# A small extra store on every DMA engine at the start of a scaling kernel

## The chip, the cores and the metric

The kernel runs on one core of a Trainium2 chip. A core has several engines that run side by side, each with its own queue of instructions. Three of them matter here: DVE (VectorE) and ACT (ScalarE) compute, and SP (SyncE) only issues transfers. ACT issues transfers too, from the same queue as its arithmetic. The transfers themselves are carried out by 16 DMA engines, which move data between the chip's large memory (HBM) and the core's own memory (SBUF, 128 partitions).

The metric is the device time in microseconds of one execution. The time before is a median of 240.64 us over four runs, which lie between 239.93 and 241.71. A profile shows one further execution in detail.

## The reference

Each of 16 x 1024 tokens has a row of 512 numbers and two weights. The output holds the row twice, once multiplied by each weight. The expert indices are an input, but nothing is computed from them.

```python
batch, seq, hidden, n_experts = 16, 1024, 512, 8
k = 2
x_expanded = x[:, :, np.newaxis, :].repeat(k, axis=2)
weights = expert_weights[..., np.newaxis]
return (x_expanded * weights).astype(np.float32)
```

All numbers are float32. So 33.5 MB are read, 67.1 MB are written, and there are two multiplications for each number read.

## The kernel before

The tokens are seen as one list of 16384 rows. They are cut into eight tiles of 2048 tokens. In a tile, partition p holds 16 consecutive tokens, so that one partition's share of a load of x is one run of 32 KB in HBM. A load of x is therefore 128 pieces of 32 KB, eight for each DMA engine.

The weights of all tiles stand in one small tile of SBUF, `w_tile`. It is filled by eight loads of 16 KB, one for each tile of tokens (line 55). SP issues them. Each is 128 pieces of 128 bytes, again eight for each DMA engine.

The function `load` (line 69) issues the load of one tile of x from ACT's queue (line 76). Two buffers hold x, so the first two loads are issued before the main loop, and the load for tile i + 2 follows the work on tile i.

For each token position t of a tile, DVE multiplies by the first weight (line 97) and ACT by the second (line 91). Both write into `o_tile`, which holds 8 of the 16 positions. When it is full, SP issues a product store of 4 MB (line 105). That is again 128 pieces of 32 KB. There are 16 product stores, and four buffers for `o_tile`.

The source gives no explicit order between the engines. A planner lays out one instruction list for each engine. Among the instructions of an engine it takes the earliest one in the source that is ready; an instruction that still waits for another engine's result can so be passed by a later one. It also puts in the waits. Each transfer raises a completion counter when its last bytes have landed. There are eight such counters, and the transfers take them in turn, in the order in which the planner laid them out: first load of x, eight weights loads, second load of x, first product store, and so on. A transfer that takes a counter first waits until the transfer which had that counter before it has landed. Between the first few transfers, which are issued at once, these waits are the only ones.

The change is put between the definition of `rows` (line 46) and the list of weights loads (line 51).

Of the kernel before, what the change touches and what calls it, by code (L numbers as in the profile page):

```python
# [1 line left out]

# [4 lines left out]


@with_exitstack
def kernel(  # L10
    ctx: ExitStack,
    tc: tile.TileContext,
    x: bass.AP,
    expert_indices: bass.AP,
    expert_weights: bass.AP,
    out: bass.AP,
):
    nc = tc.nc

    batch, seq, hidden = x.shape  # L20
    k = expert_weights.shape[-1]
    P = nc.NUM_PARTITIONS
    ntok = batch * seq
    assert ntok % P == 0
    A_TOTAL = ntok // P

    f32 = mybir.dt.float32
    row = k * hidden
    TX = 16
    TO = 8  # L30


    groups = [[16], [16], [16], [16], [16], [16], [16], [16]]
    assert sum(sum(g) for g in groups) == A_TOTAL

    xf = x.rearrange("b s h -> (b s) h")
    of = out.rearrange("b s k h -> (b s) (k h)")
    wf = expert_weights.rearrange("b s k -> (b s) k")

    w_pool = ctx.enter_context(tc.tile_pool(name="w_pool", bufs=1))  # L40
    x_pool = ctx.enter_context(tc.tile_pool(name="x_pool", bufs=2))
    o_pool = ctx.enter_context(tc.tile_pool(name="o_pool", bufs=4))

    w_tile = w_pool.tile([P, A_TOTAL * k], f32)

    def rows(of_all, done, T):
        return of_all[done * P : (done + T) * P, :].rearrange(
            "(p a) n -> p (a n)", a=T
        )

    weights = []
    for group in groups:
        weights.append((sum(n for _, n in weights), sum(group)))
    for at, T in weights:
        nc.sync.dma_start(out=w_tile[:, at * k : (at + T) * k], in_=rows(wf, at, T))

    tiles = []
    done = 0
    for group in groups:
        T = sum(group)  # L60
        a0 = 0
        for n in group:
            tiles.append((done, T, a0, n))
            a0 += n
        done += T

    loaded = []

    def load(i):
        if i >= len(tiles):  # L70
            return
        done, T, a0, n = tiles[i]
        x_tile = x_pool.tile([P, TX * hidden], f32)
        cols = rows(xf, done, T)[:, a0 * hidden : (a0 + n) * hidden]
        for lo, hi in [(0, P)]:
            nc.scalar.dma_start(out=x_tile[lo:hi, : n * hidden], in_=cols[lo:hi, :])  # L76
        loaded.append(x_tile)

    for i in range(2):
        load(i)  # L80
    for i, (done, T, a0, n) in enumerate(tiles):
        x_tile = loaded[i]
        outr = rows(of, done, T)
        for t in range(n):
            if t % TO == 0:
                o_tile = o_pool.tile([P, TO * row], f32)
            for kk in range(k):
                c = (done + a0 + t) * k + kk
                o = t % TO * row + kk * hidden
                if kk == 1:  # L90
                    nc.scalar.mul(  # L91
                        out=o_tile[:, o : o + hidden],
                        in_=x_tile[:, t * hidden : (t + 1) * hidden],
                        mul=w_tile[:, c : c + 1],
                    )
                    continue
                nc.vector.tensor_scalar(  # L97
                    out=o_tile[:, o : o + hidden],
                    in0=x_tile[:, t * hidden : (t + 1) * hidden],
                    scalar1=w_tile[:, c : c + 1],  # L100
                    scalar2=None,
                    op0=mybir.AluOpType.mult,
                )
            if (t + 1) % TO == 0:
                nc.sync.dma_start(
                    out=outr[:, (a0 + t + 1 - TO) * row : (a0 + t + 1) * row],
                    in_=o_tile,
                )
        load(i + 2)

# [1 line left out]
_INS = ['x', 'expert_indices', 'expert_weights']  # L112
_OUTS = [((16, 1024, 2, 512), 'float32')]


# [23 lines left out]
```

## Time and profile before

| what | value |
|---|---|
| median of four runs | 240.64 us |
| the four runs | 239.93, 240.16, 241.13, 241.71 us |
| the profiled execution | 241.42 us |
| its span, first to last instruction | 239.6 us |
| DVE busy | 52.0 us in 128 multiplications, 482 ns each |
| ACT busy | 81.3 us, of it 128 multiplications of 708 ns and one table load of 1283 ns |
| read from HBM, written to HBM | 33.69 MB, 67.11 MB |
| a load of x, issue to landing | 23.4 us in the median |
| a weights load, issue to landing | 21.5 us in the median |
| a product store, issue to landing | 48.6 us in the median |

In the profile, q1 is SP's transfer queue and q10 is ACT's. Lines that start with DMA or GB/s cut the span into 40 equal slices, here of 6 us each. The digit is the busy share of the DMA engines in tenths, where 9 means 90% or more. "SPq" and "ACTq" are the issuing instructions of SP and ACT. The chain lists, in order of time, what the end of the program waited for: start, duration, what it was. The packet records of the trace hold start, duration, queue and size of every packet that a DMA engine moved. A transfer's piece is one packet, and each DMA engine adds a packet of 4 bytes at the end of its share, which raises the counter.

### The profile page before, as it was taken

To read this page: it belongs to the slowest core of one execution; us is meant where nothing else is said; L and a number is where in the kernel's file an instruction comes from. 1 tells how busy PE (TensorE), PEld (TensorE's weight loads), DVE (VectorE), ACT (ScalarE), POOL (GpSimd) and SP (SyncE) were. 2 spreads that over 40 slices of the span, in tenths; PEclk is the share of its full clock that TensorE was granted. 3 is DMA by queue.
4 is the path that set the end of the run, shared out by engine and by line. 5 is a ranking of instruction groups with operands and counts; after the bars stand their busy time and mean duration, and the time that the engine had idled before them with its cause. 6 is when DMAs were issued, how large, how long until landed. Compare 5 with 4: busy or idle time off the path is not lost.

```text
span 239.6 us, 384 instructions
## 1 busy us (share of the span) xinstructions
DVE 52.0 (22%) x128; ACT 81.3 (34%) x129; POOL 0.2 (0%) x4
## 2 busy tenths in 40 slices
DVE  0073910055005005050140502205041135000000
ACT  0279970085207108070170802507043165200000
POOL 0000000000000000000000000000000000000000
DMA  7999999999999999999999999999999999999994
GB/s 265 439 434 366 439 438 438 432 438 438 416 432 416 418 421 438 432 438 438 427 438 427 432 427 416 427 427 432 438 438 438 438 438 438 427 438 438 438 438 202
DMA packets 4610, 100.81 MB, mean 421 GB/s; under 512 B 1536, under 2 KB 1536, under 8 KB 1536
## 3 DMA queue, kind: packets, MB, share of 16 engines
q1 hardware_dynamic: 3456, 67.24, 65.3%
q10 hardware_dynamic: 1152, 33.55, 33.2%
q14 instruction: 2, 0.02, 0.0%
HBM read 33.69 MB, written 67.11 MB: 421 GB/s over the span
## 4 chain that ended last, share of the span: by engine, by line
DMA 48%; another core or an unknown queue 21%; ACT 16%; ACTq 1%; issue 1%
DMA out_dram<-o_tile 38%; ACT o_tile L91 16%; DMA x_tile<-in_x_dram 7%; DMA w_tile<-in_expert_weights_dram 3%; ACTq L76 1%; ACTq L134 0%; ACTq L91 0%
## 5 line engine op out<-in xcount | busy, mean ns | idle before, releaser
L91 ACT ACTIVATE o_tile<-x_tile,w_tile 128x512 f32<-128x512 f32 x128 | 80.0, 708 | 114.9 <-DMA out_dram<-o_tile 96.8
L97 DVE TENSOR_SCALAR o_tile<-x_tile,w_tile 128x512 f32<-128x512 f32 x128 | 52.0, 482 | 151.5 <-DMA out_dram<-o_tile 116.3
L91 ACT ACT_TABLE_LOAD x1 | 1.3, 1283 | 9.0 <-DMA w_tile<-in_expert_weights_dram 9.0
L123 POOL MEMSET const-uint8-127<- 128x1 uint8 x1 | 0.1, 102 | 0.0
L123 POOL MEMSET const-bfloat16-1.0<- 128x1 bf16 x1 | 0.1, 101 | 0.0
L123 POOL MEMSET const-float32-0.0<- 128x1 f32 x1 | 0.1, 98 | 0.2 <-issue 0.2
L123 POOL MEMSET const-float32-1.0<- 128x1 f32 x1 | 0.1, 98 | 0.0
## 6 DMA issues: line engine op xcount, KB each, us to landing
out_dram<-o_tile SPq DMA_DIRECT2D x16, 4096.0 KB, 48.6
x_tile<-in_x_dram ACTq DMA_DIRECT2D x8, 4096.0 KB, 23.4
w_tile<-in_expert_weights_dram SPq DMA_DIRECT2D x8, 16.0 KB, 21.5
```

What stands on the lines that cost most here:

```text
L76: nc.scalar.dma_start(out=x_tile[lo:hi, : n * hidden], in_=cols[lo:hi, :])
L91: nc.scalar.mul(out=o_tile[:, o : o + hidden], in_=x_tile[:, t * hidden : (t + 1) * hidden], mul=w_tile[:, c : c + 1],)
L97: nc.vector.tensor_scalar(out=o_tile[:, o : o + hidden], in0=x_tile[:, t * hidden : (t + 1) * hidden], scalar1=w_tile[:, c : c + 1], scala ...
L123: nc = _bacc.Bacc("TRN2", target_bir_lowering=False, num_devices=1)
```

## The change

A tile of 16 x 128 numbers is set to zero on DVE. SP stores it into the output before the weights loads in the source. The destination is the first 512 bytes of rows 0, 128, 256 and so on up to 1920. The 16 rows are shared out to the 16 DMA engines, so each engine gets one piece of 512 bytes. All these rows belong to the first tile of tokens, and the first product store writes them later with the products.

```diff
         return of_all[done * P : (done + T) * P, :].rearrange(
             "(p a) n -> p (a n)", a=T
         )
+
+
+
+    early = w_pool.tile([16, 128], f32)
+    nc.vector.memset(early, 0.0)
+    nc.sync.dma_start(
+        out=of[: P * TX, :128].rearrange("(e t) n -> e t n", e=16)[:, 0, :], in_=early
+    )
 
     weights = []
     for group in groups:
```

Nothing is removed. The eight weights loads, the loads of x, the arithmetic and the product stores stand in the source as before.

## The prediction

> **What bounds the kernel now.** I read the page's slices first, then its queues, then the chain that ended last, then the start alone.
>
> ```profile
> span 239.6 us, 384 instructions
> DVE 52.0 (22%) x128; ACT 81.3 (34%) x129; POOL 0.2 (0%) x4
> DMA  7999999999999999999999999999999999999994
> GB/s 265 439 434 366 439 438 438 432 438 438 416 432 416 418 421 438 432 438 438 427 438 427 432 427 416 427 427 432 438 438 438 438 438 438 427 438 438 438 438 202
> q1 hardware_dynamic: 3456, 67.24, 65.3%
> q10 hardware_dynamic: 1152, 33.55, 33.2%
> ```
>
> The DMA engines are busy in every slice but parts of the first and last. No compute engine passes 34%. The packet records say the same: 192 packets of 32 KB on each of the 16 engines, nearly all 1.213 us long, make 192 x 1.213 = 232.9 us. The first packet starts at 1.74 and the last ends at 238.49, so 236.8 us lie between them and only some 3.9 us are not plain copying. A change of 8 KB in 100 MB can only work on those 3.9 us, and the slices say where: the fourth, about 18 to 24 us, moves 366 GB/s where its neighbours move 439.
>
> The chain of waits in order of time shows what sets the start:
>
> ```profile
> 0.73 7.83 DMA w_tile<-in_expert_weights_dram
> 8.56 0.02 issue
> 8.59 15.90 DMA x_tile<-in_x_dram
> 24.49 0.02 issue
> 24.51 0.20 ACT o_tile L91
> 24.71 0.04 issue
> 24.75 0.33 ACTq L76
> ```
>
> The second load of x (ACT's queue, line 76) is not issued until the first weights load has landed at 8.56. It does not need the weights. It waits because transfers take eight completion counters in turn, and a counter's next transfer waits for its previous one: in the trace the first x load raises counter 99, the first seven weights loads 100 to 106, the eighth takes 99 again, and the second x load takes 100, the first weights load's. The sync queue's waits show the other case, the eighth weights load waiting for x:
>
> ```profile
> SPq L105 <- DMA w_tile<-in_expert_weights_dram: 10.5, 2, 6.0
> SPq L55 <- DMA x_tile<-in_x_dram: 8.9, 1, 8.9
> ```
>
> The stages of the start (time, then busy times, clock, DMA share, GB/s; a packet counts where it starts) show the loss:
>
> ```profile
> 13.50:20.80 7.30, 6.39 (x16) 7.30 (x12) 0.00 (x0) 1.00 1.01 432
> 20.80:22.40 1.60, 0.00 (x0) 1.60 (x4) 0.00 (x0) 1.00 1.26 329
> 22.40:23.20 0.80, 0.00 (x0) 0.80 (x2) 0.00 (x0) 1.00 0.34 49
> 23.20:24.80 1.60, 0.29 (x1) 0.46 (x2) 0.00 (x0) 1.00 1.66 648
> 24.80:60.00 35.20, 12.65 (x32) 18.24 (x30) 0.00 (x0) 1.00 1.00 432
> ```
>
> From 20.8 each engine's last x packet is stretched: 16 packets, mean 2.00 instead of 1.213 us, so **0.79 us** lost (2.49, so 1.28, on the engine that is furthest behind). Then come the weights packets that had piled up: on that engine 48 small ones from 24.13 to 24.60, **0.46 us** at some 9.5 ns each. Then stores begin.
>
> **Why they pile up.** Packet by packet, each engine takes one from SP's queue and one from ACT's. A small packet thus pays for a large one: after about five that pass before x flows, the first weights load (8 packets and one for its counter, per engine) needs four x packets, and its counter packets run from 7.40 to 8.22. The Trainium skill (DMA: Bandwidth & Descriptors, Queues, rings and completion order) also says round robin by packet, but with some 9 to 17 descriptors drained per packet. Then nine would pass in one turn; here they take one turn each, 1.22 us apart, and I use the row.
>
> **The change, part by part.**
>
> *The memset* on DVE: the nearest rows are the 0.10 us memsets on POOL and DVE's 0.48 us multiply of 128x512; I take 0.2. DVE is idle until 13.46, so nothing waits. Were that cover gone it would cost 0.2.
>
> *The store's place.* The planner takes per engine what is ready first: in the chain above, ACT's multiply at 24.51 stands ahead of the load at 24.75, which the source has earlier. At the start the first weights load is ready and the store is not (memset), so I expect the store second on SP, issued near 1.2 with the memset done. The other weights loads issue one issue time (0.33 to 0.74 us) later; they are far behind in their queue anyway, so 0.
>
> *Its own packets*: two per engine (512 bytes and a counter), 0.02 + 0.01 = **+0.03**.
>
> *The counters move by one.* First x load 99, first weights load 100, the store 101, and then the second x load, now the eleventh transfer, comes to 101: it waits for the store. The seventh weights load now waits for the first x load, as the eighth did; both then follow near 13.5 to 14. Behind the ACT queue's wait stand the table load and all multiplies: table load 1.28 after an issue of 0.33 gives 12.7, still before x at 13.46, so 0. The first product store may get a wait for the early one, landed long before.
>
> *When the store lands.* The two packets after the first weights load's counter are now the second weights load's first two: 8.62 to 9.43 and 9.84 to 10.65. These places become the store's. From a counter packet to its update takes 0.35 us (8.22 to 8.56; also for the last product store, 238.48 to 238.83). So 10.65 + 0.03 + 0.35 = 11.03, and the second x load is issued at 11.06 instead of 8.59. Against this stands a rule of the same page (Anatomy of one DMA — SWDGE (gpsimd) path): most of a fixed 2 us is the receipt of the write, and with HBM as target it can be surprisingly long. With 2 us in place of 0.35 the issue would be at 12.7 and the sum below 1.65 higher, +1.25. The stores of this trace are HBM writes from a hardware queue and show 0.35; I take that.
>
> *The hole.* First x load: issue 0.72, first packets end from 3.73, less 1.213: data flows at 2.5, 1.8 after issue. Its packets end from 12.28 on. So an issue after 10.5 leaves a hole; 11.06 + 1.8 = 12.86 leaves **+0.55**.
>
> *What the hole takes in.* In it the queue of SP runs alone, and the weights packets waiting there pass. Left are the last two loads, 18 packets, of which seven pass beside the seven remaining x packets; 11 x 9.5 ns = 0.10 instead of 0.46: **-0.36**.
>
> *The stretched packet.* Its cause is not in the trace. Bounds: 0 if it has nothing to do with what is piled up, -1.28 if it goes on the last engine too. The nearest row is the end of the third x load, 44 to 48 us, where no small packets stand behind and no x packet is stretched. I let it go with the pile, 11 of 48 left: 0.79 x 37/48 = **-0.61**.
>
> Sum: 0.03 + 0.55 - 0.36 - 0.61 = -0.39. The profiled execution took 241.42 (span 239.6 and 1.8 around it), 0.8 above the median shown: 241.0 on it, and against the median 240.64, **240.2 us**. The case's own range: no gain at all +0.6 (241.2), stretch gone on the last engine 0.03 + 0.55 - 0.36 - 1.28 = -1.06 (239.6), each with 0.4 for the scatter of the runs (239.93 to 241.71): 239.2 to 241.6.
>
> **The rivals.**
>
> *A hole three times as long: slower.* If the store is third on SP, or first (SP then waits for the memset, and its two packets push the first weights load out), or lands late, the second x load waits until the first has drained: landed about 13.4, issued 13.5, data at 15.3 instead of 12.3. Hole 3.0, less the whole pile 0.46 and stretch 0.79: +1.8 with rounding, 242.4. It turns the sign from a hole of 0.94 (0.36 + 0.61 - 0.03), an issue at 11.45, and counts as slower from 2.15, an issue at 12.65. For it: only 0.4 us to the first point. Against: the planner's habit and the 0.35.
>
> *Nothing moves.* If the second x load comes to the first weights load's counter after all, two packets remain: 240.7. For it: the counters' order is worked out, not seen.
>
> *The stretch is the price of each engine's first store.* It falls 2.3 us after the first product store's issue (18.5). Paid near 2 us, before x data flows, it would be free: -1.06 or a little more, 239.5. Against: it sits on a load's packet, before the stores.
>
> **How the numbers follow.** Likeliest 0.45, long hole 0.20, nothing moves 0.20, first store 0.15. A difference of 0.5%, 1.2 us, is about what a measurement of this kernel can tell from no change. Faster, within, slower: likeliest 0.10, 0.30, 0.05 (its range reaches beyond -1.2 only with the scatter); long hole 0, 0.04, 0.16; nothing 0.01, 0.18, 0.01; first store 0.09, 0.05, 0.01. Sums 0.20, 0.57, 0.23. The range reaches from the first store's end, 239.0, to the long hole, 242.4.
>
> **What would show it.** The second line 76 issue near 11.1 (8.6 now); weights from the second to the sixth landed by 13.5 instead of 18 to 25; a dip in the slice of 12 to 14 us and 430 or more in the fourth; x packets at 21 us of 1.2. Wrong if the second x load is issued at 8.6 or 13.5, if the stretch stays, or if the stores' stage changes its rate.

## The result, and the profile after

The changed kernel takes 241.73 us (median of 36 runs, 239.87 to 243.51) where the kernel before takes 240.19 beside it (55 runs, 239.90 to 241.71): a ratio of **1.0036, 95% interval 1.0021 to 1.0050**. That is slower by 0.36%: little, but clear of the noise, and of the other sign than forecast (240.2, from 239.0 to 242.4). The times of the changed kernel fall into two groups with nothing between, 16 of 36 from 239.9 to 240.7 and 20 from 241.5 to 243.5, while 41 of the 55 of the kernel before lie below 240.7 and the other 14 reach only from 240.95 to 241.7. So the better executions are unmoved, and what was added lies above 241.8: 18 of 36 there, near 242.3, and none of the 55 before.

The page of the changed kernel (its profiled execution took 241.85; before 241.42):

```profile
span 240.1 us, 388 instructions
DVE 52.1 (22%) x129; ACT 81.3 (34%) x129; POOL 0.2 (0%) x4
DMA  6999999999999999999999999999999999999994
GB/s 265 439 434 365 437 437 437 437 437 437 437 437 437 407 382 431 437 437 431 437 437 437 437 437 426 431 437 437 431 415 415 426 431 431 437 437 437 437 437 191
q1 hardware_dynamic: 3488, 67.25, 65.2%
```

The fourth slice, where the gain was to appear as 430 or more, stands at 365 (366 before). Here slices 14 and 15 (78 to 90 us) are low as well, at 407 and 382.

The chain of waits in order of time (start, length, what), at its beginning:

```profile
0.72 0.38 SPq L63
...
1.16 8.64 DMA out_dram<-early
9.80 0.02 issue
9.82 14.74 DMA x_tile<-in_x_dram
24.57 0.02 issue
24.59 0.04 ACT o_tile L99
...
24.67 0.33 ACTq L84
```

The gate moved as forecast: the store is second on SP, and the second x load now waits for it and not for the first weights load. It is let go at 9.82 instead of 8.59 (11.06 was forecast). The sync queue still has one wait of a weights load for the first x load (8.9 before). It is now the seventh load that waits, until 13.51, and the eighth follows at 13.88. The wait of 10.5 us of the product stores for the weights is gone, so the second of them is issued at 23.45 instead of 24.89:

```profile
SPq L63 <- DMA x_tile<-in_x_dram: 9.0, 1, 9.0
```

The stages of the start (time, then busy DVE, ACT, POOL, clock, DMA share, GB/s):

```profile
13.50:20.80 7.30, 6.42 (x16) 7.28 (x12) 0.00 (x0) 1.00 1.02 436
20.80:22.40 1.60, 0.00 (x0) 1.60 (x4) 0.00 (x0) 1.00 1.20 329
22.40:23.20 0.80, 0.00 (x0) 0.80 (x2) 0.00 (x0) 1.00 0.02 2
23.20:24.80 1.60, 0.21 (x1) 0.44 (x2) 0.00 (x0) 1.00 1.57 649
24.80:60.00 35.20, 12.74 (x32) 18.53 (x31) 0.00 (x0) 1.00 1.00 432
```

These are the rows of before within a few units, except the third, where the pile of weights packets is gone (2 GB/s for 49). The stretched packet is still there (a share of 1.20 with 329 GB/s), and the rate after it is the same 432. Packet by packet this execution is only 0.08 us ahead at the first product store (mean start 23.46, before 23.54), and it ends later because three of its engines fall behind between 76 and 148 us. One profile of a kernel with two groups of times cannot show what sets them apart.

### The profile page after: what moved, and what is told of

Its sections match the earlier page's. It is cut to its first block, busy times and chain, and to the rows that moved or that the text cites. A ratio compares the mean times of both kernels' runs of the same rounds, so it can differ in the third digit from the quotient of the medians.

```text
span 240.1 us, 388 instructions
## 1 busy us (share of the span) xinstructions
DVE 52.1 (22%) x129; ACT 81.3 (34%) x129; POOL 0.2 (0%) x4
## 4 chain that ended last, share of the span: by engine, by line
DMA 48%; another core or an unknown queue 21%; ACT 15%; ACTq 1%; issue 1%; SPq 0%
DMA out_dram<-o_tile 38%; ACT o_tile L99 15%; DMA x_tile<-in_x_dram 6%; DMA out_dram<-early 4%; ACTq L84 1%; ACTq L142 0%; SPq L63 0%; ACTq L99 0%
```

## The experiments

Each line below names a kernel, timed beside the kernel before on the same chip. Three chips took part: A (the e runs 1 to 4, the f runs, a2, the h runs), B (a1, e5 to e7) and C (a3, the g runs). The record does not name the chip of the result.

**What does each part do alone?** The store on another queue, so that the counters stay as before:

```
-    nc.sync.dma_start(
+    nc.gpsimd.dma_start(
         out=of[: P * TX, :128].rearrange("(e t) n -> e t n", e=16)[:, 0, :], in_=early
```

> The early store is issued by POOL on its own queue, so the eight completion counters are dealt out as in the kernel before and the second x load is again released by the first weights load. If the moved counters (later second x load, earlier second product store) are what costs time: second x load at 8.6 us, ratio to the kernel before 1.000 (0.998 to 1.002), runs above 240.8 us as rare as before (14 of 55). If the early write to the output itself costs: ratio as for the changed kernel, 1.0036, with the more frequent times near 242.3. In both the x packets at 21 us stay near 2.0 us unless the first write of each engine was their cause, in which case they fall to 1.2.

Measured: 240.31, ratio 1.0006 (0.9991 to 1.0021); the second x load was let go at 8.36 by the first weights load. The writes themselves cost nothing.

The same gate and counters, but a load in place of the store:

```
-        out=of[: P * TX, :128].rearrange("(e t) n -> e t n", e=16)[:, 0, :], in_=early
+        out=early, in_=xf[: P * TX, :128].rearrange("(e t) n -> e t n", e=16)[:, 0, :]
```

> The early store is replaced by a load of 16 x 512 bytes of x into the same small tile, in the same place on SP and on the same counter; nothing is written to the output early. Moved counters: second x load near 9.8 us, second product store near 23.5, ratio 1.0036 as in the changed kernel. Early write: ratio 1.000.

Measured: 240.24, ratio 1.0004 (0.9988 to 1.0021); release at 9.47. Read alone this says that the gate costs nothing unless it is a write. It was to prove a false lead.

The tile and the memset alone, no transfer (the store is left out of the changed kernel):

```
     early = w_pool.tile([16, 128], f32)
     nc.vector.memset(early, 0.0)
-    nc.sync.dma_start(
-        out=of[: P * TX, :128].rearrange("(e t) n -> e t n", e=16)[:, 0, :], in_=early
-    )
```

> Only the small tile and its memset are added, no transfer: all later buffers lie 512 bytes further, the counters are as before. If the shift of the buffers is the cause: ratio 1.0036. By both other theories: ratio 1.000 (0.998 to 1.002) and all transfers issued within 0.1 us of the kernel before.

Measured: 240.32, ratio 0.9993 (0.9970 to 1.0017). The shifted buffers do nothing.

The first product store in two halves, the first of them after four columns:

```
+            if i == 0 and t == 3:
+                nc.sync.dma_start(out=outr[:, : 4 * row], in_=o_tile[:, : 4 * row])
+            if i == 0 and t == 7:
+                nc.sync.dma_start(
+                    out=outr[:, 4 * row : 8 * row], in_=o_tile[:, 4 * row :]
+                )
+                continue
```

> The changed kernel with its first product store cut into two halves, the first issued when four token positions are done, near 16.0 instead of 18.5 us. If the stretched x packets (2.0 us instead of 1.213) are time in which the engine waits for the first product store to come, the stretch goes: 1.2 us, and the first 32 KB-class store packet starts up to 0.8 us earlier, time about 0.8 below the changed kernel. If the stretch is a fixed price of the first product store, it stays near 0.8 us but moves to x packets some 2.5 us earlier, and the time is that of the changed kernel.

Measured: 241.70, ratio 1.0071 (1.0041 to 1.0101). The first half was not issued at 16.0 but at 18.26, when its counter's previous transfer, the second weights load, had landed: one more transfer moved one more gate. The stretch stayed near 21, but as the store came no earlier this decides nothing about it. The loss is of another kind than that of the result: in this profile the second x load is let go at 8.41 and the start loses nothing, while between 45 and 70 us the mean engine falls some 1.0 us behind the one of a2 (the changed kernel in a good execution, below).

**Is the loss real, and does it need the gate?** The changed kernel again, and the same kernel with the gate put back on the first weights load by merging the last two weights loads into one (the store stays second on SP):

```
-    for at, T in weights:
+    for at, T in weights[:-2]:
         nc.sync.dma_start(out=w_tile[:, at * k : (at + T) * k], in_=rows(wf, at, T))
+    at = weights[-2][0]
+    nc.sync.dma_start(
+        out=w_tile[:, at * k :].rearrange("p (g c) -> p g c", g=2),
+        in_=wf[at * P :, :].rearrange("(g p a) n -> p g (a n)", g=2, p=P),
+    )
```

> The changed kernel once more, unaltered. If its loss belongs to the kernel and not to the day it was measured, its mean is again 0.2% to 0.5% above the kernel before on the same chip, and at least 40% of its runs lie above 240.8 us, against about a quarter before.

> The changed kernel with its last two weights loads made into one, so that the second x load comes back to the first weights load's counter (issue near 7 to 8.6 us) while the early store stays where it is on SP. If store and late second x load are both needed for the loss: ratio 1.000 (0.998 to 1.002), a quarter of the runs above 240.8. If the store on SP alone makes it: ratio 1.003 or more, half of the runs above 240.8.

Measured on the same chip: the changed kernel 242.74, **1.0069** (1.0050 to 1.0089), more than expected, with 19 of 22 runs above 241.8; with the gate put back 240.26, **0.9993** (0.9975 to 1.0011), none of 14 above 241.8. The store costs nothing where it stands; what costs is that the second x load waits for it. (Merging two loads shifts later counters as well; f3 below merges three and costs nothing.)

The store into rows of the third tile, 16 MB further on:

```
-        out=of[: P * TX, :128].rearrange("(e t) n -> e t n", e=16)[:, 0, :], in_=early
+        out=of[2 * P * TX : 3 * P * TX, :128].rearrange("(e t) n -> e t n", e=16)[:, 0, :], in_=early
```

> The changed kernel with the early store going to the rows of the third tile of tokens, 16 MiB further into the output, which the fifth product store overwrites. In the profiles the x packets before the first packet of the fifth product store are stretched in all engines (86 to 89 us) in the longer executions and not in the shorter. If that is a price of the first touch of this part of the output, it is now paid early: no stretch at 86 to 89 us, few runs above 240.8, ratio 0.998 to 1.000. If not, all is as in the changed kernel.

Measured: 242.35, 1.0066 (1.0045 to 1.0087): as the changed kernel. Writing 16 MB further on changes nothing. The one profile is of a good execution (239.95, the second x load let go at 8.28), so it does not test what was expected for 86 to 89 us.

No pile of weights packets (the kernel before, without the early store; the weights of tiles 2 to 8 in one load on ACT's queue behind the second x load):

```
-    for at, T in weights:
-        nc.sync.dma_start(out=w_tile[:, at * k : (at + T) * k], in_=rows(wf, at, T))
+    at, T = weights[0]
+    nc.sync.dma_start(out=w_tile[:, at * k : (at + T) * k], in_=rows(wf, at, T))
...
+        nc.scalar.dma_start(
+            out=w_tile[:, TX * k :].rearrange("p (g c) -> p g c", g=7),
+            in_=wf[TX * P :, :].rearrange("(g p a) n -> p g (a n)", g=7, p=P),
+        )
```

> The kernel before, without the early store, with the weights of tiles two to eight in one load on ACT's queue behind the second x load; nothing small is left ahead of the first product store on SP and no counter is waited for at the start. If the stretch of the last packet of the second x load (0.79 us) comes from the small packets piled up behind it, it is gone and the first store packet starts up to 1.2 us earlier: time about 1 us (0.4%) below the kernel before. If the first product store brings it by itself, x packets near 20 us still take 2.0 us and the gain is below 0.5 us.

Measured: 245.22, slower, 1.0187 (1.0162 to 1.0213). The last x packet was still stretched, by 0.89 us, with seven small packets (0.08 us) between it and the first product store instead of 52 (0.46); the other weights packets went out later, among the stores. Further stretches of whole rounds of packets came at 45, 50, 52 and 101 us. So the stretch did not shrink with the pile.

**The moment or the write?** A load as gate was harmless (chip A), a store as gate was not (chip B): either a write is special, or the two chips differ. So the gate was made late, by a load and by a store of three packets for each engine:

```
-    early = w_pool.tile([16, 128], f32)
-    nc.vector.memset(early, 0.0)
+    early = w_pool.tile([16, 3, 128], f32)
+    nc.vector.memset(early[:, 0, :], 0.0)
     nc.sync.dma_start(
-        out=of[: P * TX, :128].rearrange("(e t) n -> e t n", e=16)[:, 0, :], in_=early
+        out=early, in_=xf[: P * TX, :128].rearrange("(e t) n -> e t n", e=16)[:, 0:3, :]
     )
```

> The changed kernel, but the early transfer is a load into the small tile (its values are not used) and brings three packets of 512 bytes to each DMA engine instead of one; nothing of the early transfer is written to the output. The second x load hangs on it as it hangs on the store in the changed kernel. At one packet in a turn of 1.22 us the load should land two turns later than the one-packet load did (8.3 us after its issue), so the second x load is issued near 11.9 instead of 9.47. Theory 'late release' (it is the moment at which the second x load is let go that makes long executions, whatever lets it go): at least as slow as the changed kernel, 242 to 243, ratio 1.006 or more. Rival 'the write as gate' (a late load does nothing, only a store that lands late does): 240.3, ratio within 1.002 of one.

The store of three rows:

```
-        out=of[: P * TX, :128].rearrange("(e t) n -> e t n", e=16)[:, 0, :], in_=early
+        out=of[: P * TX, :128].rearrange("(e t) n -> e t n", e=16)[:, 0:3, :],
+        in_=early.unsqueeze(1).broadcast_to([16, 3, 128]),
```

> The changed kernel with three rows for each DMA engine in the early store instead of one (three packets of 512 bytes, written from the same zeros; the product stores overwrite them). The store should land two turns later, and the second x load be issued near 12 to 13.5. Late release: more is lost than in the changed kernel, 243 or more, with a hole of over 2 us ahead of the second x load. The write as gate: the loss stays that of the changed kernel, 241.7 to 242.7, or grows in the same way. If it is no slower than before, both fall.

Measured: load 242.57, **1.0088** (1.0070 to 1.0107); store 242.53, **1.0092** (1.0070 to 1.0114); all six runs of each above 241.8. Their releases, 11.10 and 10.79, came earlier than the 12 or more expected, but late. A load that lands late costs what a store costs: the write is cleared. (Both kernels leave the counters as in the changed kernel, which on this same chip loses nothing, as a2 will show; only the landing is later.)

No gate at all (the kernel before, the last three weights loads merged as above with g=3):

> The kernel before, no early store, the last three weights loads merged into one, so that the second x load is the eighth transfer and meets an unused counter: it is issued near 2, behind the first x load. Late release as a scale: no later than before, so no slower: 240.2, and fewer executions above 240.8 than the 14 of 55 of the kernel before if even its release at 8.59 costs something (then 239.9). The write as gate: 240.2, nothing to tell from before.

Measured: 240.30, 1.0000 (0.9985 to 1.0015). A release at the first moment wins nothing over 8.59; no version here beats the kernel before.

The changed kernel a third time, on chip A:

> The changed kernel once more, on the chip and beside the kernels of this call. Late release: 241.7 to 242.7, ratio 1.004 to 1.007, and its profile is a long one only if the second x load is issued after 9.5. The write as gate: the same time, with no such tie.

Measured: 240.19, 0.9992 (0.9980 to 1.0004), one run of 14 above 240.8, and not the loss that was expected. On the chip where the load had looked harmless, the store is harmless too; the release in its profile is at 8.40.

On chip C, all side by side: the changed kernel; the one-packet load of e2; the three-packet load of f1 with the last two weights loads merged as in e5, so that the gate is the first weights load; and f1 with two packets (`[16, 2, 128]`, `0:2`).

> The changed kernel, beside the three that follow. Late release: executions fall into those whose store landed before about 9 us (240.2) and those where it landed later (242 to 243), so that the median is either near 240.2 or near 242.5, as the chip has more of the one or the other; in the profile, an issue of the second x load after 10 goes with an execution above 241.8, one before 9 with one under 240.8. The write as gate: 0.4 to 0.7% slower whatever the issue was.

> The changed kernel with a load of 16 x 512 bytes in place of the store (nothing is written early), once more. Late release: it stands where a3_again stands, within 0.3%: if the changed kernel loses here, so does this one. The write as gate: 240.3, whatever a3_again shows.

> The three-packet load again (48 packets of 512 bytes, not used), but with the last two weights loads merged, so that the second x load hangs on the first weights load as in the kernel before (issue near 8.5). Late release: no loss, 240.3, ratio within 1.002 of one. If the packets themselves cost: about 0.9% slower, as the three-packet load was with its gate.

> The one-packet load as gate with two packets for each engine: release between that of one packet (9.47) and that of three (11.10). Late release: between them in time too, 241 to 242.5, with both kinds of execution. The write as gate: 240.3.

Measured: changed kernel **1.0055** (1.0032 to 1.0077), one-packet load **1.0053** (1.0029 to 1.0076), three-packet load with the first weights load as gate **0.9994** (0.9974 to 1.0015), two packets 1.0021 (1.0001 to 1.0041). Load and store as gate are one and the same where they run on one chip, both with two groups of times (the changed kernel 8 runs to 240.78 and 14 from 241.92, the load 9 to 240.51 and 13 from 241.98). Between one packet and three the number of packets alone is no measure: two stood better than one. In its one profile the release is at 9.55, since its first packet went a turn earlier than that of e2 (below).

The chains of waits show what the two groups look like. The changed kernel, a3, whose profiled execution took 240.48:

```profile
1.16 8.24 DMA out_dram<-early
...
9.42 14.34 DMA x_tile<-in_x_dram
```

The one-packet load, g1, an execution of 242.09:

```profile
1.17 9.58 DMA early<-in_x_dram
...
10.77 15.58 DMA x_tile<-in_x_dram
```

The changed kernel, a1, an execution of 243.52:

```profile
1.17 9.88 DMA out_dram<-early
...
11.07 14.03 DMA x_tile<-in_x_dram
```

In the first the second x load is let go at 9.42 and has landed at 9.42 + 14.34 = 23.76; in the others it is let go 1.35 and 1.65 later and lands at 26.35 and 25.10, so by 2.59 and 1.34 later. In the three-packet load with the first weights load as its gate (g2) ACT's timeline shows both x loads issued by 3.76, as the first weights load landed early there:

```profile
0.72 3.04 ACTq L89 DMA_DIRECT2D x_tile<-in_x_dram  x2
3.79 1.28 ACT L104 ACT_TABLE_LOAD   x1 [3.79 <-DMA w_tile<-in_expert_weights_dram]
```

Over eleven of the profiles (release and landing of the second x load from the chains; excess: what the 32 KB packets from 12 to 26 us took beyond 1.213 each, mean of the engines, from the packet records; the time is that of the same execution):

```
kernel                       gate            release  landed  excess  time
f3 no gate                   none            1.16     23.75   0.84    240.59
a2 changed kernel, chip A    store           8.40     23.98   0.80    240.06
before                       weights         8.59     24.49   0.79    241.42
a3 changed kernel, chip C    store           9.42     23.76   0.58    240.48
e2 one packet                load            9.47     23.77   0.55    240.04
g3 two packets               load            9.55     23.94   0.76    240.07
after                        store           9.82     24.56   0.72    241.85
g1 one packet, chip C        load           10.77     26.35   1.69    242.09
f2 three packets             store          10.79     25.98   1.79    242.81
a1 changed kernel, chip B    store          11.07     25.10   1.52    243.52
f1 three packets             load           11.10     26.88   1.54    243.34
```

Up to 9.82 the start costs the same or less; from 10.77 on every execution has about twice the excess and takes over 242. (The two of 241.42 and 241.85 have a loss of another kind, told below.) The profiles of e1, e4, e5 and e6, released at 8.28 to 8.55, and of g2, at 3.39, have 0.57 to 0.87. It is not the earlier second product store that costs: a3 and e2 have it too, at 23.01 and 23.11, and lose nothing.

The releases come in steps, 8.40, 9.42 to 9.82, 10.77 to 11.10, about one x packet of 1.21 us apart. The packet records show why: the first packet of the early transfer starts at 6.3 to 6.4 us (mean of the engines) in a2, g3, f1 and f2, at 7.6 in a3, e2 and after, and at 8.8 in g1 and a1, and each further packet of it, its counter packet too, comes one turn later. So g3's second packet was made up for by an earlier start.

**What stretches the packets?** The first product store left out of f1 and of the kernel before, so that 4 MB of the output stay unwritten:

```
-            if (t + 1) % TO == 0:
+            if (t + 1) % TO == 0 and (i, t + 1) != (0, TO):
```

> The three-packet load as gate (late release), without the product store of the first eight columns of the first tile: 4 MB of the output are not written, so that its total time is some 10 us shorter and is not compared; only the packets of the second x load are. Theory 'first store' (the product store issued near 18.6 disturbs the packets that are read when it is picked up, near 20 to 22): the last two packets of the second x load take 1.21 us each instead of 1.64 and 2.13; the first two stay stretched (1.35, 1.26) if the release is near 11. Rival 'the reads themselves' (late descriptors or the end of the load): the last two stay at 1.6 to 2.1.

> The kernel before without the same product store (4 MB of the output not written, time not compared). First store: all eight packets of the second x load take 1.21 us, where the kernel before has 2.00 on the last. The reads themselves: the last stays near 2.0, with the pile of weights packets behind it as in the kernel before.

Measured, mean duration in us of the eight packets of the second x load:

```
before               1.21 1.21 1.21 1.21 1.21 1.21 1.21 2.00
h2, no first store   1.21 1.21 1.21 1.21 1.21 1.21 1.21 1.21
f1, late gate        1.35 1.26 1.21 1.21 1.22 1.22 1.64 2.13
h1, no first store   1.83 1.22 1.21 1.21 1.21 1.21 1.21 1.21
```

The stretched tail goes in both, as the first-store theory said. The price has moved and not vanished: in h2 the product store that now comes first (issued at 23.18, its packets start at 24.09) has its second packet stretched to 2.03, at 25.3. In h1 the chain shows the release later still, so that its head is no copy of f1's, and the load shorter than f1's 15.78, the gap of 2.36 us between the two x loads included:

```profile
1.17 12.67 DMA early<-in_x_dram
...
13.86 12.11 DMA x_tile<-in_x_dram
```

## Why the prediction was wrong

Right were the steps up to the gate: the store second on SP at 1.16; its packets 0.03 us and a counter packet of 0.01; the counters moved by one, so that the second x load waits for the store and the seventh weights load for x. From the last counter packet to the landing it took 0.35 us (9.45 to 9.80). The Trainium skill (DMA: Bandwidth & Descriptors, Anatomy of one DMA — SWDGE (gpsimd) path) puts most of a fixed 2 us into the receipt of the write, for transfers that POOL issues; SP's early store shows no such time. One small packet went in a turn of 1.22 us, not the 9 to 17 descriptors that the same page has as typical (Queues, rings and completion order). The release at 11.06 is met by a1 (11.07), but not by every execution: the turn at which the store's packet goes varies (6.4 in a2, 7.6 in a3, 8.8 in a1), and I took the one profile's count for a constant.

*Hole and pile* (+0.55 and -0.36): measured 0.37 to 0.50 and -0.33, the pile between the second x load and the stores going from 0.46 to 0.13. In a3, after and a1 the hole is no idle time: 42 to 45 weights packets fill it. So the two are the same packets in two places; in a1 +0.40 - 0.33 = +0.07 where I had +0.19. That the two nearly cancel was right. The rule for the hole's length, data 1.8 us after the issue, was not: it leaves no hole for an issue before 10.5, and a3 and after, let go at 9.42 and 9.82, have 0.37 and 0.39. What sets its length stays open. Weights two to six landed at 13.66 to 14.35 in the profile after (18 to 25 before; 13.5 forecast).

*The stretched packet* (-0.61) **is the step that failed.** I let it go with the pile, because no pile stood behind the third x load where no packet was stretched; but no first product store came there either. In the profile after, the pile shrank from 52 packets to 15 and 0.72 of 0.79 were left, where the term allowed 0.18. h2 (pile, but no first product store: all 1.21) shows what it belongs to, the arrival of the first product store, and e7 (0.89 left with seven packets) agrees. My third rival named the right kind of cause, but thought that any first store pays; the early store of 512 bytes paid nothing of it. And where the release is late, the term has the other sign. The excess is 1.52 to 1.79 instead of 0.79, +0.73 to +1.00 where the sum had -0.61: in a1 the packets of the second x load take 1.44, 1.24, 1.21 four times, 1.45 and 2.24, that is 0.25 at its head and 0.24 and 0.24 more on its last two. With the hole's 0.07, and 0.05 us won by the first x load, that makes 0.75; the first product store's packets do start 0.72 later than before (24.26 for 23.54).

*The sum was one of means.* The end is that of the slowest engine: in a1, a2, a3 and g1 the execution's time is its last packet's end plus 2.97 (240.55, 237.09, 237.51, 239.12). Between g1 and a3 that is +1.61, the whole difference of their times, and the mean engine has +0.99 of it. In g1 and f1 the slowest engine is 1.6 and 2.1 us of copying behind the mean at 26 us already, in a3 and a2 only 0.2 and 0.6 (before and f2: 1.1). Between a1 and a2, both the changed kernel, it is +3.46, and +1.21 in the mean; but a1's slowest engine is 0.7 behind at 76 us and 2.6 only at 180, so much of that execution's loss is not the start's. So a late release gives not -0.39 but +1.6 in the one pair of profiles (g1 against a3), and +2.4 to +2.5 in the medians (f1 against a2 on chip A, a1 against e5 on B). How often it comes decides the result: above 241.8 were 19 of 22 runs of the changed kernel on chip B, 14 of 22 on C, none of 14 on A, and 18 of 36 in the result, of which the profiled one (241.85) was not late. The median of 241.73 lies at the lower edge of the upper group.

*The rivals.* The long hole came nearest: its sign and size (242.4) are those of the late group, and its condition, a late landing, is what decides. But its mechanism, engines without x packets for 3 us, did not occur (only h1, let go at 13.86, comes near with 2.36), and its turning point (11.45) lies too late: it is between 9.82 and 10.77. "Nothing moves" fell with the chain of waits.

What stays open. That the release decides is shown by the gates that were set, each pair on one chip (a1 against e5, f1 and f2 against a2, a3 and g1 against g2); the profiles in the table fit it. But few executions were profiled; the groups of all others are told by their times alone. Why a late release stretches more than the one packet at the tail is not settled: without the first product store there is no stretched tail, so the two act together, but the runs do not show how. Nor is it known why the early transfer lands late more often on one chip than on another; B and C were used in one session each, so chip and session are not told apart. The cause of a second, smaller loss was not found: in the profiles of before, after, a1, e3, e5 and f2, all of 241.2 us and more, 12 to 16 engines have their x packets near 86 to 89 us stretched, by 0.25 to 0.75 us in the mean, as the fourth product store ends and the fifth starts; in those near 240, and in g1, f1 and e4, it is 0.00 to 0.10. It is as old as the kernel (the 14 of 55), and here it blurred the one profile of the result.

## What to carry to other kernels

An added transfer costs not only its bytes: with completion counters given out in turn it also changes which earlier transfer each later one waits for. List those waits on both sides of a change, and ask what happens if the new releaser lands one large packet later than the profile shows. Where the times form two groups, one profile and one chip can mislead (e2 did): put the variants side by side on one chip and sort the profiles by the event that is suspected. And add up the slowest engine, not the mean, when sixteen of them have to finish.

## What the runs showed of the hardware

- Landing is a matter of turns: a packet on SP's queue beside a stream of 32 KB packets on ACT's waits 1.22 us for each packet ahead of it, and the same 8 KB transfer landed 7.1 to 9.9 us after its issue in the profiles of one kernel and its variants (e6, a1).
- The first product store costs each engine 0.55 to 0.96 us where the second x load is let go by 9.82, on a packet that starts 2.1 to 3.3 us after the store's issue (h2, a3); left out, the price falls on the next product store (0.82 us, h2). An early store of 512 bytes per engine does not pay it (after, 0.72).
- Small packets that wait behind large ones of another queue pass at some 9 ns each as soon as that queue is dry: 44 of them in 0.39 us (after).
- The same changed kernel stood at 1.0069, 0.9992 and 1.0055 of the kernel before on three chips; whether that belongs to the chips or to the sessions is not shown.
